# One transformer-like layer on one core: the Hyena filter's layers are placed ahead of the adaLN products in the first stage

## The chip, the cores and the metric

The kernel runs on one core of one Trainium2 chip. A core has five engines that run side by side, each with its own instruction queue, which it works off strictly in order: PE (TensorE, the matrix products), DVE (VectorE), ACT (ScalarE), POOL (GpSimd) and SP (SyncE, which here only issues transfers from memory to the core). The metric is the time of one execution on the device, in microseconds (us). Three executions of the kernel before took 1778.08, 1781.75 and 1783.15 us, so the median is 1781.75 us.

## The reference

The reference is one layer of a hybrid backbone over 512 latent tokens of width 1024, with 256 context tokens. Cut to what the change touches:

```python
mod = (silu(c) @ w_ada + b_ada).reshape(B, 1, 6, D)          # adaLN: shift, scale, gate, twice
xn = rmsnorm(x, norm_mix_g) * (1 + mod[:, :, 1]) + mod[:, :, 0]
cn = rmsnorm(ctx, norm_mix_g) * (1 + mod_c[:, :, 1]) + mod_c[:, :, 0]
p, pc = xn @ w_in, cn @ w_in                                  # one projection feeds three mixers
# the Hyena filter depends on weights alone, not on x
h = sin(freq[0] * (z @ f1_w + f1_b))                          # z: a table of positions, 512 x 33
h = sin(freq[1] * (h @ f2_w + f2_b))
h = (h @ f3_w).reshape(L, 2, 256) * decay[:, None, :]
K = rfft(concat(h[:, 0], 0, flip(h[1:, 1])))                  # used by the long convolution
# the RG-LRU's decay, from a parameter alone
log_a = -8 * r * softplus(-lam)
```

After this come neighbourhood attention, the Hyena convolution, the RG-LRU, a gated merge, an expert retrieval (PEER) over 16384 experts and a last RMSNorm.

## The kernel before, in words

The code is written once as a long program; a scheduler then sets, at build time, the order in which each engine gets its instructions (it moves an instruction ahead of others when it expects its inputs to be there), and the engines work off those fixed lists, waiting on semaphores. So the place of a piece of code moves work in the lists, but not one to one.

Activations lie transposed, as 8 blocks (index k, 0 to 7) of 128 features by 512 tokens. A product in full precision is made of three: each operand is split into a high part and a rest (`wh`, `wl` of a weight, `xh`, `xl` of the input), and `wh xh`, `wh xl`, `wl xh` are summed.

The first stage (before.py, lines 324 to 500) is one loop over k. Round k does the following.

- `mods(k)` (L422 to L439): two weight blocks `ada` of 512 KB each arrive (four buffers, so two rounds' worth), 8 products each of `silu(c)` with them go to the PSUM tile `hx`, ACT copies the result to `rows`, two small products with `pick` (L434) sum the partial rows, and DVE adds the bias (`mod`, L435) and makes the scale `gsx` (L437).
- In round 0 the input `xT` (four transfers of 512 KB) is squared on ACT (L298), summed on DVE (L300), summed over partitions by one product with `onesm` (L306), and turned into `rx`, one over the root mean square, by `rstd_of` (L231 to L237).
- In rounds 0 to 3 the weights of four of the input projection's column blocks arrive (`win`, 512 KB each) and are split by ACT and DVE.
- `norm_k` (L309 to L313): DVE scales `xT[k]` (L311), ACT adds the shift (`xh`, L312), DVE makes the rest (`xl`, L313).
- `part(k - 3)` (L443 to L447): the 12 products of input block k - 3 with those four weight blocks, 512 columns each. They accumulate over k in four PSUM tiles, so none is finished before `part(7)`.
- `filt()` (L371 to L411) is a generator that makes the Hyena filter in four pieces, one for each `next(fl)`: the first sine layer (L373, `sine` L335 to L349), the second (L377, and `softplus_rows`, a polynomial of some 25 tiny DVE operations for the RG-LRU), the third layer times the decay table (`hf`, `hp`, `hm`, L386 to L393), and the Fourier tables `Kf` (16 products of `dft` with the table `dftf`, L320, then L399 to L410). Before, the pieces run in rounds 1, 3 and 5 (`FS`) and after the loop. It uses `hx` tiles too, of which there are two.

After the loop, ACT copies the four finished tiles to `ha` (L271), ACT and DVE normalise the context, and the projections, the Hyena convolution and the RG-LRU begin. SP issues all transfers of the stage in one list; at most eight are under way, and a ninth waits for the landing of the first (the wait stands in SP's list).

Of the kernel before, what the change touches and what calls it, by code (L numbers as in the profile page):

```python
# [23 lines left out]
KD = 8  # L24
# [15 lines left out]
NFIRST = 4  # L40
SEQ1 = "hhhhrrhrrhhrhrhrhh"
SEQ2 = "vvvvrkrkrkrk"
FS = (1, 3, 5)
CS = 5
XK = 0
CL = 3
DL = 4
LAG = 3
NGR = 4
TWO_PI = 2.0 * math.pi  # L50
# [105 lines left out]
def emit(ctx, tc, A, out, dbg=None):  # L156
    nc = tc.nc
# [99 lines left out]
    dftf = hc.tile([128, 4, 2, 256], F32, name="dftf")  # L257
# [45 lines left out]
    def stats(npl, src, n):  # L303
        acc = ssq(npl, src, n)
        pss = hx.tile([128, 512], F32, name="hx")[:, :n]
        PE.matmul(pss, onesm, acc, start=True, stop=True)  # L306
        return rstd_of(npl, pss, n)
# [15 lines left out]
    with ExitStack() as st:  # L323
# [4 lines left out]
        zT = fp.tile([64, T], F32, name="zT")  # L328
        f1 = fp.tile([64, 64], F32, name="f1")
        f2 = fp.tile([64, 64], F32, name="f2")  # L330
# [20 lines left out]
        def softplus_rows():  # L351
            y = fp.tile([128, 4], F32, name="spy")
            z = fp.tile([128, 4], F32, name="spz")
            z2 = fp.tile([128, 4], F32, name="spz2")
            pl = fp.tile([128, 4], F32, name="spp")
            S.activation(y, vec("rlam"), AF.Abs)
            S.activation(y, y, AF.Exp, scale=-1.0)
            V.tensor_scalar(z, y, 2.0, None, ALU.add)
            V.reciprocal(z, z)
            V.tensor_mul(z, z, y)  # L360
            V.tensor_mul(z2, z, z)
            V.memset(pl, 1.0 / 19)
            for c in range(17, 0, -2):
                V.tensor_mul(pl, pl, z2)
                V.tensor_scalar(pl, pl, 1.0 / c, None, ALU.add)
            V.tensor_mul(pl, pl, z)
            V.tensor_scalar(y, vec("rlam"), -1.0, 0.0, ALU.mult, ALU.max)
            V.scalar_tensor_tensor(out=pl, in0=pl, scalar=2.0, in1=y, op0=ALU.mult, op1=ALU.add)
            V.tensor_scalar(nsp, pl, -8.0, None, ALU.mult)

        def filt():  # L371
            p = hx.tile([128, 512], F32, name="hx")
            PE.matmul(p[:64], f1, zT, start=True, stop=True)  # L373
            h1 = sine(p[:64], 0, vec("f1b")[:64])
            yield
            p = hx.tile([128, 512], F32, name="hx")
            PE.matmul(p[:64], f2, h1, start=True, stop=True)  # L377
            h2 = sine(p[:64], 1, vec("f2b")[:64])
            softplus_rows()
            yield  # L380
            hp = fp.tile([128, 4, 256], F32, name="hp")
            hm = fp.tile([128, 4, 256], F32, name="hm")
            for j in range(4):
                p = hx.tile([128, 512], F32, name="hx")
                o_ = j // 2 + 256 * (j % 2)
                PE.matmul(p, h2[:, o_:o_ + 255:2], f3, start=True, stop=True)  # L386
                hf = fp.tile([128, 2, 256], F32, name="hf", bufs=2)
                V.tensor_tensor(hf, p.rearrange("p (d c) -> p d c", d=2),
                                dec[:, j].unsqueeze(1).to_broadcast([128, 2, 256]), ALU.mult)
                if j == 0:  # L390
                    V.memset(hf[0:1, 1], 0.0)
                V.tensor_add(hp[:, j], hf[:, 0], hf[:, 1])
                V.tensor_sub(hm[:, j], hf[:, 1], hf[:, 0])  # L393
            yield
            for f in range(2):
                X, Y = hx.tile([128, 512], F32, name="hx"), at.tile([128, 512], F32, name="at")
                dft(X, Y, f, hp, hm)
                Ys = fp.tile([128, 512], F32, name="Ys", bufs=1)
                S.activation(Ys, Y, AF.Copy, scale=wf[:, f:f + 1])  # L399
                for i, op in enumerate((ALU.add, ALU.subtract)):  # L400
                    V.scalar_tensor_tensor(out=Kf[:, f, i, 0:512], in0=X, scalar=wf[:, f:f + 1], in1=Ys, op0=ALU.mult, op1=op)
                    if f == 0:
                        V.memset(Kf[0:1, 0, i, 256:512], 0.0)
                    S.copy(Kf[:, f, i, 512:768], Kf[:, f, i, 0:256])
                if f == 0:
                    V.tensor_scalar(Kq[:, 1], Ys[0:1, 256:512], 2.0, None, ALU.mult)
            p = hx.tile([128, 512], F32, name="hx")
            for k in range(2):
                PE.matmul(p[:32, :256], dftf[:, k, 1, 0:32], hp[:, k], start=k == 0, stop=k == 1)
            V.tensor_scalar(Kq[:, 0], p[0:1, :256], 2.0 / 1024, None, ALU.mult)  # L410
            yield  # L411

        fl = filt()
# [29 lines left out]
        def part(k):  # L443
            for i, (ps, wh, wl) in enumerate(first):
                PE.matmul(ps, wh[:, k], xh[:, k], start=k == 0, stop=False)
                PE.matmul(ps, wh[:, k], xl[:, k], start=False, stop=False)
                PE.matmul(ps, wl[:, k], xh[:, k], start=False, stop=k == KD - 1)  # L447

        for k in range(KD):
            lda = mods(k)  # L450
            if k == XK:
                for q in range(0, KD, 2):
                    nc.sync.dma_start(xT[:, q:q + 2], A["xT"][:, q:q + 2])
                rx = stats(npl, xT, T)
            if k == XK:
                for t_, n in ((zT, "zT"), (f1, "f1w"), (f2, "f2w"), (f3, "f3w")):
                    nc.sync.dma_start(t_, A[n])
            if k < NFIRST:
                src = A["win"][(14, 16, 15, 17)[k]]
                if k < 2:  # L460
                    w = load_raw(src)
                    wh, wl = (t[:, :, k * 128:k * 128 + 128] for t in (ch, cl))
                    S.copy(wh, w)
                    V.tensor_sub(wl, w, wh)
                else:
                    wh, wl = load_split(src)
                ps = (pj.tile([128, 512], F32, name="pj") if k < 2 else at.tile([128, 512], F32, name="at") if k == 2
                      else at.tile([128, 512], F32, name="po", bufs=1))
                first.append((ps, wh, wl))
            for q in (range(k + 1) if k == XK else [k] if k > XK else []):  # L470
                norm_k(xT, q, 0, gsx, rx, xh, xl)
            if k >= LAG:
                part(k - LAG)
            with tc.issue_after(lda.ins):
                if k == CL:
                    nc.sync.dma_start(cT, A["ctxT"])
                if k == DL:
                    nc.sync.dma_start(dec, A["dec"])
                if k == KD - 1:
                    for t_, n in ((wf, "wf"), (dftf, "dftf")):  # L480
                        nc.sync.dma_start(t_, A[n])
            if k in FS:
                next(fl)
            if k == CS:
                rc = stats(npl, cT, CT)
                V.tensor_tensor(cT, cT, rc.unsqueeze(1).to_broadcast([128, KD, CT]), ALU.mult)
# [830 lines left out]
```

## Time and profile before

| what | value |
|---|---|
| median of three runs | 1781.75 us (1778.08 to 1783.15) |
| the profiled execution's own time | 1777.03 us |
| its span, first to last instruction | 1774.9 us |
| what lies around the span | 2.1 us |
| PE busy | 1731.8 us (98%) |
| DVE, ACT, POOL busy | 1372.9, 788.6, 357.9 us |
| PE idle in all | 43.1 us |
| PE busy in the first 23 us | 9.35 us |
| mean granted TensorE clock | 0.995 |

The profiled execution is a run of its own, 4.7 us below the median and a little below the fastest of the three timed runs. The busy time of PE is modelled at the ends of products, so that a PE shown as full can still have small holes. The page names lines as they stand in before.py. In the changed file, lines from L44 on stand one to four lower or higher: the filter's L373 is L372 there, `mods` L429 is L427, `pick` L434 is L432, `part` L445 to L447 are L443 to L445.

### The profile page before, as it was taken

How to read it: one execution, taken by the hardware profiler on the slowest of the kernel's cores; microseconds unless marked ns; L12 is line 12 of the kernel's file. 1: busy time of each engine (PE TensorE's matmuls, PEld its weight loads, DVE VectorE, ACT ScalarE, POOL GpSimd, SP SyncE). 2: the span in 40 equal slices, each digit the busy share in tenths (PEclk: the TensorE clock that was granted, in tenths of full speed). 3: DMA queues.
4: the chain of work that ended last, by engine and by line, in shares of the span. 5: the costliest groups of instructions: out<-in, count | busy, mean ns of one | idle time of the engine just before them, and what ended most of it. 6: DMA issues, size and time to landing. Idle time of an engine off the chain costs nothing.

```text
span 1774.9 us, 25755 instructions
## 1 busy us (share of the span) xinstructions
PE 1731.8 (98%) x9601; PEld 1523.8 (86%) x9601; DVE 1372.9 (77%) x2555; ACT 788.6 (44%) x1140; POOL 357.9 (20%) x268
## 2 busy tenths in 40 slices
PE   6999999999999999999999999999999999999997
PEld 4778888888877889999999888888888888888885
DVE  7675666664448999999886787888888888788887
ACT  5545563343334235567766433333333333333334
POOL 0000000000000001100010233434434434444441
PEclk9999999999999999999999999999999999999999
DMA  9311155552343225767868999999999999999984
GB/s 343 105 60 60 48 167 172 186 172 87 119 163 119 84 86 189 257 223 287 290 253 323 376 353 344 338 330 341 337 353 341 348 343 349 332 345 339 321 287 150
DMA packets 157677, 431.33 MB, mean 243 GB/s; under 512 B 12784, under 2 KB 62192, under 8 KB 155504
## 3 DMA queue, kind: packets, MB, share of 16 engines
q1 hardware_dynamic: 116224, 257.44, 42.6%
q0 software_dynamic: 36864, 134.23, 20.9%
q10 hardware_dynamic: 4464, 38.01, 5.5%
q8 instruction: 75, 1.23, 0.3%
q14 instruction: 50, 0.41, 0.1%
HBM read 388.48 MB, written 41.16 MB: 242 GB/s over the span
## 4 chain that ended last, share of the span: by engine, by line
PE 85%; DVE 7%; DMA 4%; ACT 3%; issue 1%; SPq 0%; ACTq 0%; DVEq 0%
PE ac L1231 10%; PE ac L1232 10%; PE ac L1233 10%; PE pS L226 8%; PE pS L225 8%; PE pS L224 8%; PE pj L224 6%; PE pj L225 6%; PE pj L226 6%; DVE wl L218 2%; PE po L793 1%; PE pG L1104 1%; PE pG L1105 1%; PE hx L224 1%; PE hx L226 1%; PE hx L225 1%
## 5 line engine op out<-in xcount | busy, mean ns | idle before, releaser
L217 ACT CAST wh<-wraw 128x1024 fp32r<-128x1024 f32 x340 | 350.6, 1031 | 442.7 <-PE pS L225 227.2
L218 DVE TENSOR_TENSOR wl<-wraw,wh 128x1024 fp32r<-128x1024 f32 x340 | 406.7, 1197 | 140.3 <-ACT wh L217 138.8
L1132 POOL DMA_INDIRECT gr<-u_rows,idx x128 | 168.9, 1319 | 942.0 <-DVE db L1037 481.6
L226 PE MATMUL pS<-zh,wl 128*128 128x384 f32 x1024 | 345.6, 338 | 1.2 <-DVE wl L218 1.2
L224 PE MATMUL pS<-zh,wh 128*128 128x384 f32 x1024 | 344.7, 337 | 0.0
L225 PE MATMUL pS<-zl,wh 128*128 128x384 f32 x1024 | 344.6, 337 | 0.0
L1232 PE MATMUL ac<-wl,ah 128*128 128x512 f32 x768 | 299.0, 390 | 0.0
L1233 PE MATMUL ac<-wh,al 128*128 128x512 f32 x768 | 298.9, 389 | 0.0
L1231 PE MATMUL ac<-wh,ah 128*128 128x512 f32 x768 | 292.0, 389 | 0.0
L1142 POOL DMA_INDIRECT gr<-v_rows,idx x128 | 177.6, 1388 | 212.0 <-DVE yacc L1148 177.2
L224 PEld LDWEIGHTS pS<-zh,wh 128*128 128x128 f32 x1024 | 192.4, 188 | 3.0 <-ACT wh L217 0.5
L226 PEld LDWEIGHTS pS<-zh,wl 128*128 128x128 f32 x1024 | 192.3, 188 | 2.6 <-DVE wl L218 2.1
L225 PEld LDWEIGHTS pS<-zl,wh 128*128 128x128 f32 x1024 | 192.5, 188 | 2.3
L1233 PEld LDWEIGHTS ac<-wh,al 128*128 128x128 f32 x768 | 144.2, 188 | 30.0
L1231 PEld LDWEIGHTS ac<-wh,ah 128*128 128x128 f32 x768 | 144.2, 188 | 27.9
L1232 PEld LDWEIGHTS ac<-wl,ah 128*128 128x128 f32 x768 | 144.2, 188 | 27.8
L1148 DVE SCALAR_TENSOR_TENSOR yacc<-gr,cf,yacc 128x1024 f32<-128x1024 f32 x126 | 159.7, 1280 | 8.7 <-DMA gr<-v_rows,idx 8.6
L1134 DVE SCALAR_TENSOR_TENSOR gr<-gr,xtk 128x1024 f32<-128x1024 f32 x128 | 154.8, 1219 | 4.6 <-DMA gr<-u_rows,idx 4.6
L224 PE MATMUL pj<-xh,wh 128*128 128x512 f32 x336 | 134.8, 401 | 3.0 <-DVE ql L751 1.7
L226 PE MATMUL pj<-xh,wl 128*128 128x512 f32 x336 | 133.7, 398 | 1.0 <-DVE wl L218 1.0
L225 PE MATMUL pj<-xl,wh 128*128 128x512 f32 x336 | 133.8, 398 | 0.0
L1107 ACT COPY stg<-pG 128x512 f32<-128x512 f32 x96 | 99.4, 1164 | 23.9 <-PE pG L1105 23.7
(394 smaller groups left out, 2572.2 us busy)
## 6 DMA issues: line engine op xcount, KB each, us to landing
wraw<-u_cols SPq DMA_DIRECT2D x128, 512.0 KB, 6.3
wraw<-v_rows SPq DMA_DIRECT2D x128, 512.0 KB, 6.6
Gd<-stg ACTq DMA_DIRECT2D x12, 2048.0 KB, 8.9
gt<-Gd SPq DMA_DIRECT2D x32, 768.0 KB, 10.1
wraw<-wada SPq DMA_DIRECT2D x32, 512.0 KB, 4.4
wraw<-wgate SPq DMA_DIRECT2D x24, 512.0 KB, 3.5
Sd<-sg ACTq DMA_DIRECT2D x15, 768.0 KB, 4.9
sgl<-Sd SPq DMA_DIRECT2D x15, 768.0 KB, 7.9
```

The source lines that it names most:

```text
L217: S.copy(h[:, :k], r[:, :k])
L218: lsub[0] = V.tensor_sub(l[:, :k], r[:, :k], h[:, :k])
L224: PE.matmul(ps, wh[:, kw], xh[:, kx], start=start and j == 0, stop=False)
L225: PE.matmul(ps, wh[:, kw], xl[:, kx], start=False, stop=False)
L226: PE.matmul(ps, wl[:, kw], xh[:, kx], start=False, stop=stop and j == n - 1)
L1132: GP.indirect_dma_start(out=r, out_offset=None, in_=A["u_rows"], in_offset=bass.IndirectOffsetOnAxis(ap=idx3[:, j:j + 1], axis=0))
L1134: V.scalar_tensor_tensor(out=r, in0=r, scalar=1.0, in1=xtk, op0=ALU.mult, op1=ALU.mult, accum_out=sel3[:, j:j + 1])
L1142: GP.indirect_dma_start(out=r, out_offset=None, in_=A["v_rows"], in_offset=bass.IndirectOffsetOnAxis(ap=idx3[:, j:j + 1], axis=0))
L1148: V.scalar_tensor_tensor(out=a, in0=r, scalar=cf3[:, j:j + 1], in1=a, op0=ALU.mult, op1=ALU.add)
L1231: PE.matmul(ac[t][h], ah[:, ts], vhf[:, hs_], start=j == 0, stop=False)
L1232: PE.matmul(ac[t][h], ah[:, ts], vlf[:, hs_], start=False, stop=False)
L1233: PE.matmul(ac[t][h], al[:, ts], vhf[:, hs_], start=False, stop=j == NB - 1)
```

## The change

Four things change in the text of the first stage. The filter's small inputs (`zT`, `f1w`, `f2w`, `f3w`: 128, 16, 16 and 128 KB) are issued ahead of everything but `sv`. The decay table `dec` (512 KB), `wf` (1 KB) and the table `dftf` (1024 KB) are issued right behind `xT`, instead of behind the adaLN weights of rounds 4 and 7. The filter's four pieces run ahead of round 0, in round 0, and in rounds 1 and 3. `softplus_rows` leaves the second piece and is written in round 5.

```diff
-FS = (1, 3, 5)
+FS = (1, 3)
 CS = 5
 XK = 0
 CL = 3
-DL = 4
...
             h2 = sine(p[:64], 1, vec("f2b")[:64])
-            softplus_rows()
             yield
...
+        for t_, n in ((zT, "zT"), (f1, "f1w"), (f2, "f2w"), (f3, "f3w")):
+            nc.sync.dma_start(t_, A[n])
+        next(fl)
         for k in range(KD):
             lda = mods(k)
             if k == XK:
                 for q in range(0, KD, 2):
                     nc.sync.dma_start(xT[:, q:q + 2], A["xT"][:, q:q + 2])
+                next(fl)
                 rx = stats(npl, xT, T)
-            if k == XK:
-                for t_, n in ((zT, "zT"), (f1, "f1w"), (f2, "f2w"), (f3, "f3w")):
+                for t_, n in ((dec, "dec"), (wf, "wf"), (dftf, "dftf")):
                     nc.sync.dma_start(t_, A[n])
...
                 if k == CL:
                     nc.sync.dma_start(cT, A["ctxT"])
-                if k == DL:
-                    nc.sync.dma_start(dec, A["dec"])
-                if k == KD - 1:
-                    for t_, n in ((wf, "wf"), (dftf, "dftf")):
-                        nc.sync.dma_start(t_, A[n])
             if k in FS:
                 next(fl)
+            if k == CS:
+                softplus_rows()
```

What the scheduler made of it is seen in the engines' lists. From the end of the first context projection on, all lists are the same in both kernels, and no instruction is added; one table load of ACT is gone (the second L233). Three places matter.

SP's list from the start (`sv` is a table of small vectors, `wada` the adaLN weights, `win` the input projection's). Before:

```order
L176 DMA sv<-sv 128x156
L426 DMA ada<-wada 128x1024 x2
L453 DMA xT<-xT 128x1024 x4
L457 DMA zT<-zT 64x512
L457 DMA f_127<-f1w 64x64
L457 DMA f_128<-f2w 64x64
L457 DMA f_129<-f3w 64x512
L208 DMA wraw<-win 128x1024
L426 DMA ada<-wada 128x1024 x2
```

Changed:

```order
L175 DMA sv<-sv 128x156
L448 DMA zT<-zT 64x512
L448 DMA f_127<-f1w 64x64
L448 DMA f_128<-f2w 64x64
L448 DMA f_129<-f3w 64x512
L424 DMA ada<-wada 128x1024 x2
L454 DMA xT<-xT 128x1024 x4
L458 DMA dec<-dec 128x1024
L458 DMA wf<-wf 128x2
L458 DMA dftf<-dftf 128x2048
L207 DMA wraw<-win 128x1024
L424 DMA ada<-wada 128x1024 x2
```

Four small transfers now stand ahead of the first adaLN weights, and 1.5 MB of tables ahead of the first projection weights.

DVE's list while it sums the squares of `xT` (`sqa` the sum, `sk` and `sa` the sine's steps, `spp` and `nsp` the polynomial). Before:

```order
L435 TENSOR_TENSOR mod<-hx,sv 128x2x2
L300 TENSOR_TENSOR sqa<-sqa,sq 128x512
L368 SCALAR_TENSOR_TENSOR spp<-spp,spy 128x4
L437 SCALAR_TENSOR_TENSOR gsx<-mod,sv 128x1
L300 TENSOR_TENSOR sqa<-sqa,sq 128x512
L369 TENSOR_SCALAR nsp<-spp 128x4
L300 TENSOR_TENSOR sqa<-sqa,sq 128x512 x5
L464 TENSOR_TENSOR cl<-wraw,ch 128x8x128
```

Changed:

```order
L299 TENSOR_TENSOR sqa<-sqa,sq 128x512 x2
L433 TENSOR_TENSOR mod<-hx,sv 128x2x2
L340 TENSOR_SCALAR sk<-sa 64x512
L435 SCALAR_TENSOR_TENSOR gsx<-mod,sv 128x1
L341 TENSOR_SCALAR sk<-sk 64x512
L299 TENSOR_TENSOR sqa<-sqa,sq 128x512
L344 SCALAR_TENSOR_TENSOR sa<-sk,sa 64x512
L299 TENSOR_TENSOR sqa<-sqa,sq 128x512
L344 SCALAR_TENSOR_TENSOR sa<-sk,sa 64x512
L299 TENSOR_TENSOR sqa<-sqa,sq 128x512
L345 TENSOR_SCALAR sa<-sa 64x512
L299 TENSOR_TENSOR sqa<-sqa,sq 128x512 x2
```

The second sine layer's five steps now stand between the sums of the squares; the polynomial still stands ahead of both, as before, and the first sine layer's five steps now stand among its operations.

PE's list at the end of the stage (the last rows of `part(6)`, then `pick` of round 7, then the first rows of `part(7)`). Before:

```order
L446 MATMUL po<-xl,wh 128x512
L447 MATMUL po<-xh,wl 128x512
L320 MATMUL hx<-hp,dftf 128x256 x2
L320 MATMUL hx<-hm,dftf 128x256 x2
L320 MATMUL hx<-hp,dftf 128x256 x2
L320 MATMUL hx<-hm,dftf 128x256 x2
L445 MATMUL pj<-xh,ch 128x512 x2
```

Changed, first behind `part(3)` and then at the end:

```order
L444 MATMUL po<-xl,wh 128x512
L445 MATMUL po<-xh,wl 128x512
L427 MATMUL hx<-ada,ha_113 32x128 x32
L432 MATMUL hx<-pick,rows 128x2 x4
L305 MATMUL hx<-sqa,onesm 128x256
L427 MATMUL hx<-ada,ha_113 32x128 x16
L443 MATMUL pj<-xh,ch 128x512 x2
```

```order
L444 MATMUL po<-xl,wh 128x512
L445 MATMUL po<-xh,wl 128x512
L432 MATMUL hx<-pick,rows 128x2 x2
L443 MATMUL pj<-xh,ch 128x512 x2
```

Before, `pick` of round 7 stands inside `part(6)` and eight filter products lie between it and `part(7)`; now nothing lies between. And `mods` of rounds 4, 5 and 6 stand together ahead of `part(4)`.

## Rows read from the trace of the kernel before

**Rows 1.** Busy time by stretch: us, PE busy, PEld, DVE, ACT, POOL, clock, DMA share, GB/s.

```profile
23.00:72.00 49.00, 47.63 (x348) 33.26 (x344) 34.69 (x76) 20.96 (x37) 0.00 (x0) 0.97 0.53 198
101.00:1775.00 1674.00, 1650.12 (x9050) 1465.52 (x9048) 1302.11 (x2378) 735.76 (x1051) 357.17 (x262) 1.00 0.70 245
```

**Rows 2.** The chain that ended last, 0 to 120 us: start, us, what.

```profile
4.21 9.29 DMA xT<-xT
13.51 6.65 DMA wraw<-win
...
69.60 0.23 PE pj L447
```

**Rows 3.** DMA issues up to 60 us: times issued, KB, us from issue to landing.

```profile
dftf<-dftf SPq DMA_DIRECT2D x1, 1024.0 KB, 7.0
...
f<-f3w SPq DMA_DIRECT2D x1, 128.0 KB, 7.9
sv<-sv SPq DMA_DIRECT2D x1, 78.0 KB, 1.9
```

**Rows 4.** Timeline of SP's queue: start, us taken to issue, what.

```profile
4.82 0.56 SPq L457 DMA_DIRECT2D zT<-zT  x1
```

**Rows 5.** Timeline, start of the stage: start, us, instruction, [idle before <-what ended it].

```profile
8.83 0.63 ACT L298 ACTIVATE sqa<-xT 128x512 f32<-128x512 f32 x1
...
15.79 2.07 PE L306 MATMUL hx<-sqa,onesm 128*128 128x512 f32 x2 [5.79 <-DVE sqa L300]
...
23.17 1.22 PE L445 MATMUL pj<-xh,ch 128*128 128x512 f32 x2
```

**Rows 6.** DVE's groups up to 75 us: times run | busy us, mean ns | idle before.

```profile
L311 DVE SCALAR_TENSOR_TENSOR xT<-xT,gsx,rs_r 128x512 f32<-128x512 f32 x8 | 6.0, 748 | 0.2
L300 DVE TENSOR_TENSOR sqa<-sqa,sq 128x512 f32<-128x512 f32 x7 | 4.8, 691 | 0.5 <-ACT sq L298 0.2
L218 DVE TENSOR_TENSOR wl<-wraw,wh 128x1024 fp32r<-128x1024 f32 x3 | 3.6, 1215 | 0.7 <-ACT wh L217 0.7
L300 DVE TENSOR_TENSOR sqa<-sqa,sq 128x256 f32<-128x256 f32 x7 | 2.9, 415 | 0.3
L345 DVE SCALAR_TENSOR_TENSOR sa<-sk,sa 64x512 f32<-64x512 f32 x4 | 2.7, 677 | 0.0
L388 DVE TENSOR_TENSOR hf<-hx,dec 128x512 f32<-128x512 f32 x4 | 2.7, 687 | 3.6 <-PE hx L386 3.6
L392 DVE TENSOR_TENSOR hp<-hf 128x256 f32<-128x256 f32 x4 | 1.7, 421 | 0.0
L435 DVE TENSOR_TENSOR mod<-hx,sv 128x4 f32<-128x4 f32 x8 | 1.3, 158 | 3.1 <-PE hx L434 3.1
L341 DVE TENSOR_SCALAR sk<-sa 64x512 f32<-64x512 f32 x2 | 0.8, 414 | 0.4 <-ACT sa L340 0.4
```

**Rows 7.** Timeline, end of the stage (a product of 32-bit floats is listed as two).

```profile
60.00 1.08 PE L429 MATMUL hx<-ada,ha 128*32 128x128 f32 x32
...
62.55 0.50 PE L434 MATMUL hx<-pick,rows 128*128 128x2 f32 x4
...
64.71 0.71 ACT L312 ACTIVATE xh<-xT,mod 128x512 fp32r<-128x512 f32 x1
64.84 1.03 PE L320 MATMUL hx<-hp,dftf 128*128 128x256 f32 x4
...
68.11 0.81 PE L445 MATMUL pj<-xh,ch 128*128 128x512 f32 x2
```

**Rows 8.** Tile `ada`, its one transfer issued at 42.8 us into an idle queue.

```profile
DMA to landing us min/median/max: 3.7/3.7/3.7
```

**Rows 9.** Busy time by stretch, at the two falls of the clock (columns as Rows 1).

```profile
90.67:94.08 3.41, 0.89 (x8) 0.70 (x6) 3.41 (x7) 1.53 (x2) 0.00 (x0) 1.00 0.44 154
94.08:100.91 6.83, 6.41 (x17) 4.88 (x18) 5.10 (x13) 1.83 (x3) 0.00 (x0) 0.50 0.21 77
22.40:25.81 3.41, 3.41 (x35) 1.92 (x28) 3.41 (x9) 2.10 (x4) 0.00 (x0) 0.50 1.02 410
```

## Prediction

> **What bounds the kernel now.** I read first the busy time by stretch. Behind the first stage PE is busy 1650 of 1674 us [rows 1]: what follows runs PE's list, which the change leaves as it is, so a stage that ends later or earlier should move the end by as much. From 23 to 72 us PE is nearly full too, 47.6 of 49 us [rows 1]; the room lies ahead of 23 us. I then read the chain of waits: up to 20.2 us it is made of transfers, `xT` until 13.5 us and projection weights behind it [rows 2], then of PE with short pieces of DVE and ACT. Last I read the timeline at both ends of the stage. PE waits 5.8 us for the sum of the squares, which is there at 15.8 us, and `part(0)` begins at 23.2 us [rows 5]; `part(7)` begins at 68.1 us [rows 7]. So the question is what the change does to these two times.
>
> **Head of SP's queue.** Four small transfers move ahead of the adaLN weights. One took 0.56 us to issue [rows 4]; four make 2.2 us, so the first weights land some 2 us later. Their data are in time for PE's first filter product: `sv`, alone in the queue, took 1.9 us [rows 3]. The tables `dec` and `dftf` (1.5 MB) move ahead of the first projection weights; at the 410 GB/s of the full queue [rows 9] they take 3.8 us. Those weights thus land about 3 to 4 us later than before, near 20 us. That is not what decides, as the next part shows.
>
> **DVE sums the squares later.** This is the main cost. A sine layer is five DVE operations: two of 0.68 us and three of 0.41 [rows 6], together 2.6 us. Two of them now stand ahead of the end of the sum. The first runs among the polynomial's operations; ACT's sine stands in ACT's list ahead of the copy `rows` and the squares, so the first square, at 8.8 us before [rows 5], moves to about 12.2. From the first sum, at 13.5, DVE has seven sums of 0.69, the second layer's 2.6 us and two operations of 0.16: 7.7 us, so the sum is there at 21.4 us, not 15.8. From there to `part(0)` it took 7.4 us before [rows 5]. The table load and the weight split of ACT that lay in it are now partly done by then, so I take 6.5: `part(0)` begins at 27.9 us, 4.7 later. Bounds: 1.5 later, if ACT's sine is out early enough for the squares to keep up with `xT`, and 7 later, if the late weights hold ACT as well.
>
> **DVE's next stretch.** Between DVE's first scaling of `xT` (about 27.1 us) and round 2's `mod` now lie the filter's third layer and the context's squares: 4 `hf` of 0.69, 8 `hp` and `hm` of 0.42, three weight splits of 1.2, three operations of `norm_k` of 0.75, seven sums of 0.42 and six small ones of 0.16 [rows 6], in all 15.9 us: until 43.0. PE's own list to that point is shorter: 24 products of `part(0)` and `part(1)` at 0.23 us [rows 2], two rounds of `mods` of 1.1, eight Fourier products of 0.41 (eight took from 64.84 to 68.11 us) [rows 7] and three of the third layer, twice as wide, of 0.8: 13.4 us, until 41.3. So the other Fourier products, which need `hx` tiles that this `mod` frees, begin at about 43.2.
>
> **PE from there.** Eight Fourier products, 3.3; `part(2)` and `part(3)`, 5.5; two narrow products for `Kq`, 0.8; `mods` of rounds 4 and 5, 2.2; four rows of `pick` and the context's sum, 1.2: 56.2 us. Now round 6's `mods` come, and their weights can be issued only when round 4's have been read, from 53.3 us on. A transfer into an idle queue lands 3.7 us after its issue [rows 8], so they come at 57.0, the second half 1.3 us behind: PE waits 1.5 us in all and is through at 58.9. `part(4)` and `part(5)`, `pick`, round 7's `mods` and `part(6)` take 9.7: 68.6. Then `pick` of round 7, and `part(7)` must wait for DVE and ACT to make `xh` of it: 2.9 us from the start of `pick` (62.55) to the end of `xh` (65.42) before [rows 7]. Before, eight Fourier products covered this; they are gone from there, so it stands open: 71.5 us. By the same prices the old stretch from 23.2 to 68.1 comes to 40 us and took 44.9; the rest is a low clock and small holes. I have counted most waits by name, so I add 1.4, about a third of that rest, as an estimate. **`part(7)` begins at 72.9 instead of 68.1 us: 4.8 us later.** Bounds: 0 (no such rest, an early sum) and 9.
>
> **Behind it.** The last filter work (`Kf` on DVE, its copies on ACT, `Kq` on PE) is gone from behind `part(7)`. DVE and ACT were waiting for each other there, so I take no gain, and let a gain of 1 us widen the low side. The polynomial still heads DVE's list, the saved table load lay where ACT waited; both count nothing.
>
> The sum is +4.8 us on the profiled execution: 1777.0 to 1781.8. That execution lies 4.7 us under the median, so for the median I say 1781.75 + 4.8 = **1786.5 us**, 0.27% more. About 0.3% (5.3 us) is what a measurement of this kernel can tell from no change, so this is, narrowly, no change.
>
> **Rivals.**
> 1. *The clock falls at a new wait* (slower). Ahead of `part(7)` PE now waits 2.5 us. Before, PE had 0.89 us of work between 90.7 and 94.1 us, waiting for the rest, and the granted clock was 0.50 (1.2 GHz) for the next 6.8 us [rows 9]. The 12 products of `part(7)` would then take 0.43 us each instead of 0.23: 2.4 us more, +7.2 in all, 1789 us. It decides if the new wait is as bare as that one; the 1.5 us at `mods` are broken by eight products. At 22.4 us the clock was low as well [rows 9], and that stays. The Trainium skill (TensorE: Matmul & The Clock Gate, section HAM oscillation) says that waits of the products for data bring the clock down again; by that rule the trace agrees at 94 us, and this rival would hold.
> 2. *The early start comes true* (lower). If the sines fit into DVE's holes and ACT's squares follow `xT`, `part(0)` begins near 23.2 as before, with the second layer and one third-layer product (0.8 us each) already done, and `Kq` (0.8) no longer behind `part(7)`: about -2.5 us; with the low clock at 22.4 and the wait near 94 us also gone, up to -7, 1775 us. For it: PE is idle early. Against: DVE runs its list in order, and the sums stand behind the sines.
> 3. *Each small transfer pays its whole latency in turn.* `sv` alone took 1.9 us [rows 3]; four in a row would hold the first weights 7.6 us instead of 2.2, +10.2, 1792 us. Against it: before, the last of the four, issued behind the others, landed 7.9 us after its issue [rows 3], under 2 us behind the last `xT`; so they overlap. The Trainium skill (DMA: Bandwidth & Descriptors, section Anatomy of one DMA) states, for GpSimd's path, a fixed cost of about 2.0 us per transfer, which speaks against small ones in front. By it the four would cost 8 us if they did not overlap; the trace does not bear that out.
> 4. *Nothing moves.* The polynomial is not moved in DVE's list at all, and if transfers alone set the stage, the order of the rest is indifferent: 0, 1782 us.
>
> **Chances.** The forecast (+2 to +7, 1783.5 to 1789) 0.53, a third of it above 5.3 us; rival 1, 0.22; rival 2, 0.12, a third of it beyond -5.3; rival 3, 0.03; rival 4, 0.10. So slower by over 0.3%: 0.18 + 0.22 + 0.03 = 0.43. Faster: 0.04. Same: 0.53. The range from 1779 to 1791.5 us leaves out most of rival 2, rival 3 and the outer end of rival 1.
>
> **What would show it.** In the changed profile the sum's product (`onesm`) should start near 21, not 15.8 us, behind DVE; `part(0)` near 28; `mods` of round 6 should wait for a transfer, and the first product of `part(7)` for ACT's `xh`, about 2.5 us, starting near 73; the first stage's delay should be found again, unchanged, at 101 us and at the end. I am wrong if `part(0)` begins before 25 us, if `part(7)` begins before 69, or if the delay there is not that at the end. A clock of 0.50 between 70 and 80 us would be rival 1.

## The result and the profile after

The changed kernel takes 1791.3 us in the median of six runs (1787.5 to 1797.5), the kernel before, run beside it, 1781.0 us (1778.1 to 1783.2). The ratio is 1.0063, with a 95% interval of 1.0046 to 1.0080: 11 us slower, between 8 and 14. The prediction was 4.8 us, 1786.5. A second set of six runs gave 1793.4 us against 1780.1, ratio 1.0068 (1.0053 to 1.0083), 12 us.

The profiled execution took 1797.5 us, the slowest of its six; its span is 1795.4 us, PE was busy 1745.2 us. The profiled execution of the kernel before, 1777.0 us, lay a little below its timed runs, so the two are 20 us apart, twice what the medians are: the rows show where time goes, the medians how much it is. First the chain of waits up to `part(0)` (start, us, what), to be read against [rows 2]:

```profile
4.33 5.17 DMA ada<-wada
...
9.52 10.23 DMA wraw<-win
...
19.78 1.04 ACT ch L464
...
20.84 1.28 ACT L232
22.13 0.70 ACT rs_r L232
...
25.82 0.73 ACT xh L311
...
26.59 1.18 PE pj L443 x2
```

SP issues the first projection weights only when an adaLN block has landed (9.5 us), they land at 19.75 us (before, ACT's split of them began at 16.35), ACT splits them (`ch`), loads its table and only then makes `rs_r`. `part(0)` begins at 26.6 instead of 23.2 us [rows 5], and the 3.4 us are those of the landing (19.75 against 16.35). The sum of the squares, which the prediction had held responsible, is late as well, but not last. The timeline of PE (start, us, instruction, [idle before <-what ended it]):

```profile
19.70 2.07 PE L305 MATMUL hx<-sqa,onesm 128*128 128x512 f32 x2 [5.78 <-DVE sqa L299]
...
23.63 1.13 PE L384 MATMUL hx<-f,sh 64*128 64x512 f32 x2
...
26.59 1.18 PE L443 MATMUL pj<-xh,ch 128*128 128x512 f32 x2 [1.29 <-ACT xh L311]
27.70 2.07 PE L384 MATMUL hx<-f,sh 64*128 64x512 f32 x2
...
48.55 1.11 PE L319 MATMUL hx<-hp,dftf 128*128 128x256 f32 x4
...
63.72 0.66 PE L427 MATMUL hx<-ada,ha 128*32 128x128 f32 x16 [1.25 <-DVE xT L310]
64.87 1.08 PE L427 MATMUL hx<-ada,ha 128*32 128x128 f32 x16 [0.49 <-DMA ada<-wada]
...
81.24 1.21 PE L443 MATMUL pj<-xh,ch 128*128 128x512 f32 x2 [2.42 <-ACT xh L311]
...
104.91 0.64 PE L544 MATMUL hx<-ident,hu 128*128 128x128 f32 x4
```

The sum's product ends at 21.8 us; the two paths to `rs_r` end within 0.4 us of each other. The waits for round 6's weights (1.25 and 0.49 us; DVE, which the first row names, had long been done) and for `xh` ahead of `part(7)` (2.42 us) are there as predicted. But `part(7)` begins at 81.2 us, 13.1 later than before [rows 7], and the first transposes of the Hyena convolution (`ident,hu`) at 104.9 instead of 90.9 us. Two rows of the kernel before for this, from its timeline:

```profile
16.35 1.04 ACT L463 CAST ch<-wraw 128x1024 fp32r<-128x1024 f32 x1 [1.62 <-DMA wraw<-win]
...
90.92 0.64 PE L546 MATMUL hx<-ident,hu 128*128 128x128 f32 x4
```

The rest is in the clock. Busy time by stretch (us, PE, PEld, DVE, ACT, POOL busy, granted clock, DMA share, GB/s), cut where the clock changed; the stretches left out are at 1.00:

```profile
23.26:26.67 3.41, 2.12 (x23) 1.08 (x15) 3.31 (x5) 2.14 (x3) 0.00 (x0) 1.00 1.02 399
26.67:40.33 13.66, 13.66 (x22) 6.33 (x23) 11.23 (x24) 4.57 (x8) 0.00 (x0) 0.50 0.78 306
...
64.22:71.05 6.83, 6.34 (x35) 4.70 (x29) 0.87 (x2) 0.59 (x2) 0.00 (x0) 0.50 0.36 143
...
81.29:84.70 3.41, 3.41 (x8) 2.74 (x9) 3.38 (x4) 0.51 (x1) 0.00 (x0) 0.50 0.00 0
```

From 26.7 to 40.3 us PE is busy without a break and at half rate (1.2 GHz); before, the low stretch there was 3.4 us long [rows 9]. Among the products of this stretch stand three of the third layer's four, whose operands fill 64 of the 128 rows (`64x512`; each product is listed as two): 2.07 us, as at 27.70. The first of the four took 1.13 us (23.63), for the clock had been up from 23.3 us; it fell behind the wait of 1.29 us ahead of `part(0)`. Two further low stretches stand behind the two later waits. (Ahead of the first record of the clock, here up to 23.3 us, the column says 1.00 in every kernel; a pair of 512-column products that takes 2.07 us, as at 19.70, shows the lower level, since it takes 1.02 to 1.13 at 1.00.) A second profile of the same kernel has no record of the clock ahead of 42.8 us, with products at half rate up to there, and again a fall at each wait:

```profile
66.69:73.51 6.82, 6.20 (x31) 4.75 (x29) 0.75 (x1) 0.45 (x2) 0.00 (x0) 0.50 0.34 137
...
83.75:87.17 3.42, 3.42 (x8) 2.74 (x9) 3.39 (x4) 0.51 (x1) 0.00 (x0) 0.50 0.00 0
```

### The profile page after: what moved, and what is told of

Same layout as the page of the kernel before. It is cut to its first block, busy times and chain, and to the rows that moved or that the text cites. A ratio compares the mean times of both kernels' runs of the same rounds, so it can differ in the third digit from the quotient of the medians.

```text
span 1795.4 us, 25752 instructions
## 1 busy us (share of the span) xinstructions
PE 1745.2 (97%) x9601; PEld 1532.0 (85%) x9601; DVE 1373.1 (76%) x2555; ACT 787.6 (44%) x1139; POOL 353.6 (20%) x268
## 4 chain that ended last, share of the span: by engine, by line
PE 89%; DMA 5%; DVE 4%; ACT 2%; issue 1%; SPq 0%; DVEq 0%; ACTq 0%
PE ac L1229 9%; PE ac L1230 9%; PE ac L1231 9%; PE pS L225 9%; PE pS L223 9%; PE pS L224 9%; PE pj L223 6%; PE pj L225 6%; PE pj L224 6%; PE pG L1102 1%; PE po L791 1%; PE hx L223 1%; PE pG L1103 1%; PE hx L224 1%; PE hx L225 1%; DVE wl L217 1%
```

## The experiments

Each kernel was timed in 5 to 12 runs beside the kernel before, in four sets; "x us slower" is the ratio's value on 1780 us.

**The changed kernel again** (`after_again`), no edit.

> The changed kernel once more, for a second profile. Theory 'delay': the first stage is late by the order of the work alone (sines between the sums, wait before part(7)); a profile with no more low clock than the kernel before then has part(7) at 72 to 74 us and a time of 1785 to 1787 us, and the profile at hand (part(7) at 81.2) was one bad execution. Theory 'clock': TensorE, left with less to do early, stays at half rate to about 40 us in every execution; then the products of part(0) and of the third layer again take 0.43 us and 2.07 us for two, the granted clock is 0.50 for over 10 us ahead of 42 us, part(7) comes at 76 to 82 and the time is 1789 to 1793 us.

1793.4 us; the two rows above are its own, `part(7)` at 83.7 us. The early low clock stands in both profiles, and theory "delay" falls; `part(7)` and the time lie a little beyond what "clock" had said.

**Transfers alone** (`transfers_only`), against the kernel before:

```diff
+        for t_, n in ((zT, "zT"), (f1, "f1w"), (f2, "f2w"), (f3, "f3w")):
+            nc.sync.dma_start(t_, A[n])
         for k in range(KD):
...
                 rx = stats(npl, xT, T)
-            if k == XK:
-                for t_, n in ((zT, "zT"), (f1, "f1w"), (f2, "f2w"), (f3, "f3w")):
+                for t_, n in ((dec, "dec"), (wf, "wf"), (dftf, "dftf")):
                     nc.sync.dma_start(t_, A[n])
```

(and `dec`, `wf`, `dftf` no longer issued in rounds 4 and 7)

> Only the transfers of the change (four small ones ahead of the adaLN weights, the two tables ahead of the projection weights); the four pieces of the filter and the polynomial stay where they were. Theory 'delay' and theory 'clock' both say the transfers are not what costs: xT lands 1.2 us later than before, the sum's product starts near 17, part(0) at 24 to 25, part(7) near 69.5, time 1782 to 1784 us. Rival 'transfers': the later projection weights (19.8 instead of 16.3 us) set the stage; then part(0) is at 26 to 27 and the time 1786 to 1791 us.

1785.0 us, ratio 1.0028 (1.0015 to 1.0040), 5 us slower. The timeline of ACT and PE, then the stretch behind the clock's first recorded rise:

```profile
11.59 0.37 ACT L432 COPY rows<-hx 128x256 f32<-128x256 f32 x1 [7.00 <-PE hx L429]
...
18.73 2.08 PE L306 MATMUL hx<-sqa,onesm 128*128 128x512 f32 x2 [5.71 <-DVE sqa L300]
...
20.85 0.69 ACT L233 ACTIVATE rs_r<-hx,eps 128x512 f32<-128x512 f32 x1 [1.79 <-PE hx L306]
...
26.32 0.79 PE L445 MATMUL pj<-xh,ch 128*128 128x512 f32 x1 [0.28 <-ACT xh L312]
```

```profile
36.37:390.00 353.63, 345.33 (x1982) 289.66 (x1975) 228.33 (x367) 172.50 (x301) 3.61 (x2) 1.00 0.37 119
```

The transfers do cost, and `part(0)` is where the rival had it, at 26.3 us; the time lies between the two forecasts. The path is another one than in the changed kernel: the adaLN weights are late, ACT's squares stand in its list behind the copy `rows` that needs them, the sum comes 2.9 us later than before without any sine in front of it, and here `rs_r` waits for the sum, not for the projection weights. The clock is up from 36.4 us only. So 3 us of late start need no sine layer.

**Sine layers alone** (`sines_only`), against the kernel before:

```diff
-FS = (1, 3, 5)
+FS = (5,)
...
+        next(fl)
         for k in range(KD):
...
+                next(fl)
                 rx = stats(npl, xT, T)
```

(the four small transfers stand at the head here too)

> Only the two sine layers go early (with their four small transfers at the head); the tables, the third layer and the Fourier products stay in their old rounds, so eight Fourier products again stand between the last pick and part(7). Theory 'delay': the sum's product at 20 to 21 us, part(0) near 27, no wait before part(7), which starts at 71 to 72: 1784.5 to 1786 us. Theory 'clock': the same order, but the products of the rounds behind 27 us run at half rate to about 40 us as in the changed kernel: part(7) at 74 to 77, 1788 to 1791 us.

1782.9 us, ratio 1.0018 (1.0007 to 1.0029), 3 us slower. The sum's product starts at 21.2, `part(0)` at 28.8 us, later than in the changed kernel, and yet this one costs least, less than either theory had said. Its low stretch is short (busy time by stretch):

```profile
29.02:32.43 3.41, 3.41 (x22) 2.04 (x22) 3.27 (x9) 1.45 (x2) 0.00 (x0) 0.50 1.00 381
32.43:97.28 64.85, 60.01 (x402) 45.64 (x400) 40.11 (x84) 29.08 (x55) 0.00 (x0) 1.00 0.43 157
```

**Fourier tables back behind the loop** (`fourier_last`), against the changed kernel:

```diff
-FS = (1, 3)
+FS = (1,)
```

> The changed kernel with its last filter piece (Fourier tables) asked for behind the loop again, as before; the order on PE then has eight Fourier products in the middle of the stage and eight and the two narrow ones behind part(7). Theory 'delay': the same sum near 19.7 and part(0) near 26.6 as in the changed kernel; 4 us of work leave the place ahead of part(7) and come behind it; the wait of 2.4 us for xh stays: time within 2 us of the changed kernel's. Theory 'clock': the low stretches of the changed kernel's start (26.7 to 40.3) are there too, so no more than 2 us are won either. Rival 1 of the prediction (the wait before part(7) decides): if that wait is gone here, 2.5 to 5 us are won.

1784.8 us, ratio 1.0023 (1.0013 to 1.0032), 4 us slower than before and 8 faster than the changed kernel of the same set. The scheduler put eight Fourier products back ahead of `part(7)`, and the waits for the weights and for `xh` are gone (timeline of PE, then busy time by stretch):

```profile
66.55 1.08 PE L427 MATMUL hx<-ada,ha 128*32 128x128 f32 x32 [0.33 <-DVE mod L433]
...
74.88 0.82 PE L443 MATMUL pj<-xh,ch 128*128 128x512 f32 x2
```

```profile
41.77:103.20 61.43, 55.80 (x440) 44.95 (x440) 35.45 (x74) 29.23 (x53) 0.00 (x0) 1.00 0.36 129
```

The early half rate is there as before the edit (to 41.8 us); no fall follows until 103 us. Both theories had given 2 us at most: they had missed that the cover comes back. Rival 1 had 2.5 to 5 us for that case, and 8 is more than the two waits make (4.2 us). The two low stretches behind the waits are gone as well; they held 9.75 us of PE's work at half rate (6.34 and 3.41 in the first profile), so at 1.00 some 4.9 us less, by an estimate from these rows. That the remainder is this is not shown.

**Keeping PE busy early** (`warm_after`), against the changed kernel; nothing is left out, the added products go into a PSUM tile that is overwritten later (they are written out here; the kernel has them in a small helper function):

```diff
+        for _ in range(5):
+            PE.matmul(po0[:, :128], onesm, onesm, start=True, stop=True)
         next(fl)
+        PE.matmul(po0, f3[:, :128], zT, start=True, stop=True)
...
                 next(fl)
+                for q in (4, 5, 6, 7):
+                    PE.matmul(po0[:, :256], onesm, xT[:, q, :256], start=True, stop=True)
                 rx = stats(npl, xT, T)
```

> The changed kernel with products added whose result nobody reads, in TensorE's early waits (five while the first transfers come, one behind the first filter product, four on xT ahead of the sum); every engine's list is otherwise the same. Theory 'clock' (TensorE is at its lower level to about 42 us because it had too little to do before): the products of part(0) and part(1) take 0.23 instead of 0.43 us, the Fourier products behind them start at 43 to 46 instead of 48.6 and 51 us, and the kernel is 3 to 6 us faster than the changed one: 1787 to 1790 us. Theory 'delay' (DVE's list sets the pace there): at most 1 us is won, 1792 us or more.

1790.4 us, ratio 1.0054 (1.0038 to 1.0070): 1 to 3 us under the changed kernel, inside the uncertainty of both. The clock did rise, and fell again (busy time by stretch):

```profile
17.69:21.10 3.41, 1.12 (x2) 0.30 (x2) 1.78 (x4) 1.37 (x3) 0.00 (x0) 1.00 1.01 407
21.10:41.58 20.48, 19.04 (x60) 9.15 (x61) 16.23 (x29) 9.41 (x15) 0.00 (x0) 0.50 0.81 317
```

It was up at 17.7, with PE busy 1.1 of the next 3.4 us it went down, and it then stayed down for 20.5 us although PE was busy for 19.0 of them. So too little early work alone does not hold it down to 41 us; something in those 20 us does.

**Filling the wait ahead of `part(7)`** (`fill7`), and **both additions** (`warm_fill`: this edit and that of `warm_after`), against the changed kernel:

```diff
                                    op0=ALU.add, op1=ALU.mult)
+            if k == KD - 1:
+                for _ in range(3):
+                    PE.matmul(ps[:, 260:508], onesm, rows[:, :248], start=True, stop=True)
             return ld
```

> The changed kernel with three products of 248 columns added between the last pick and part(7), in the wait for xh, whose result nobody reads. They can't shorten the wait. Rival 1 of the prediction (the clock falls at this wait): the granted clock stays 1.00 behind it, the products of part(7) take 0.23 us instead of 0.43, 1.5 to 2.5 us are won, about 1791 us. If the wait alone costs: no difference to the changed kernel (1793 us), or 0.5 us more for what the added products hold up.

> Both additions at once. Theory 'clock': the gains add up, 5 to 8 us off the changed kernel, 1785 to 1788 us, which leaves the 3 to 5 us over the kernel before that the order alone costs. Theory 'delay': not under 1791 us.

`fill7`: 1792.1 us, ratio 1.0064 (1.0047 to 1.0081); `warm_fill`: 1792.5 us, ratio 1.0056 (1.0039 to 1.0074). Neither differs measurably from the changed kernel. In `fill7`'s profile the filling worked (timeline of PE, then busy time by stretch):

```profile
78.05 1.52 PE L439 MATMUL hx<-rows,onesm 128*128 128x248 f32 x6 [0.32 <-DVE mod L433]
80.15 0.73 PE L446 MATMUL pj<-xh,ch 128*128 128x512 f32 x2 [0.57 <-ACT xh L311]
```

```profile
67.80:105.35 37.55, 32.24 (x193) 26.30 (x191) 22.40 (x44) 20.03 (x34) 0.00 (x0) 1.00 0.25 85
```

The clock stayed at 1.00 behind the wait, and no gain is seen: the wait for `xh` itself remains. The fall behind it would cost 1.7 us (3.41 us of work at half rate, an estimate), and the interval of 3 us to either side can neither show nor exclude that. In `warm_fill`'s profile the early low stretch stood again, to 41.4 us.

**The kernel before, kept busy early** (`warm_before`) and **filled in its own wait near 92 us** (`before_fillhu`, two products of 512 columns between the two groups of `ident,hu`), each against the kernel before (the first again written out):

```diff
+        for _ in range(10):
+            PE.matmul(po0[:, :128], onesm, onesm, start=True, stop=True)
         for k in range(KD):
...
                     nc.sync.dma_start(xT[:, q:q + 2], A["xT"][:, q:q + 2])
+                for q in range(8):
+                    PE.matmul(po0[:, :256], onesm, xT[:, q, :256], start=True, stop=True)
```

```diff
         for c in range(2):
             p = hx.tile([128, 512], F32, name="hx")
+            for _ in range(2 * c):
+                PE.matmul(p, onesm, us[0], start=True, stop=True)
```

> The kernel before with such products in the same waits (ten while the first transfers come, eight on xT; the scheduler then also shifts a few products of the rounds 0 to 3). Theory 'clock': it too was held at half rate ahead of 26 us; the sum's product takes 1.1 instead of 2.1 us, the eight-product groups of mods 0.5 instead of 1.1, and 2 to 4 us are won: 1776 to 1778 us. Rival: transfers and DVE set the pace there, the PE work at half rate was hidden, 0 to 1 us.

> The kernel before with two added products (512 columns, result unread) in its own wait for hu at 91.6 to 94.2 us, behind which the granted clock was 0.50 for 6.8 us. Theory 'clock': the clock stays 1.00 there, the 17 products behind take 0.23 instead of 0.43 us, 2 to 3.4 us are won: 1777 to 1778.5 us. Rival: DVE, which is late there, sets the pace, and nothing is won: 1780 to 1781 us.

1779.9 us, ratio 1.0001 (0.9990 to 1.0013), and 1779.6 us, ratio 0.9997 (0.9985 to 1.0010): nothing won. In the first the clock was up from 6.7 us, but fell for 6.8 us at 20.4; in the second it stayed up behind that wait. A low stretch taken away is not time won in these two places.

**Third layer padded to 128 rows** (`pad128`), against the changed kernel; the added rows are zero:

```diff
-        f3 = fp.tile([64, 512], F32, name="f3")
+        f3 = fp.tile([128, 512], F32, name="f3")
+        V.memset(f3[64:], 0.0)
+        h2p = fp.tile([128, T], F32, name="h2p")
+        V.memset(h2p[64:], 0.0)
...
-            h2 = sine(p[:64], 1, vec("f2b")[:64])
+            sine(p[:64], 1, vec("f2b")[:64], h2p[:64])
+            h2 = h2p
...
```

> The changed kernel with the third layer's two operands padded with zeros from 64 to 128 rows; PE's list is the same. In the changed kernel these four products (2.07 us each at half rate) stand among the products of part(0) and part(1), and the clock is at its lower level to 40 to 43 us though TensorE is busy without a break from 27 us on, also where it had been kept busy before. Theory 'narrow products' (it is these products of 64 rows that keep the clock low): the granted clock is 1.00 by 31 to 35 us, the Fourier products behind start 3 to 5 us earlier, 1787 to 1790 us. Rival 'only time' (the rows don't matter): low to 40 us or more again, 1790 to 1794 us.

1785.5 us, ratio 1.0028 (1.0018 to 1.0039): 5 us slower than before instead of 12. This is the experiment that decides. The lists of PE, ACT and SP are, but for the padded operand's name, those of the changed kernel; DVE's has two memsets more and a few set-up operations of the first 5 us in another order. Busy time by stretch, then the timeline of PE:

```profile
23.13:98.22 75.09, 63.78 (x479) 49.55 (x479) 50.12 (x100) 35.51 (x64) 0.00 (x0) 1.00 0.48 174
```

```profile
24.29 1.13 PE L388 MATMUL hx<-f,h2p 128*128 128x512 f32 x2 [0.59 <-DVE rs_t L233]
...
31.48 1.02 PE L388 MATMUL hx<-f,h2p 128*128 128x512 f32 x2
...
42.53 1.11 PE L319 MATMUL hx<-hp,dftf 128*128 128x256 f32 x4
...
57.72 0.65 PE L431 MATMUL hx<-ada,ha 128*32 128x128 f32 x16 [1.26 <-DVE xT L310]
...
72.42 0.73 PE L447 MATMUL pj<-xh,ch 128*128 128x512 f32 x2 [2.42 <-ACT xh L311]
94.90 0.64 PE L548 MATMUL hx<-ident,hu 128*128 128x128 f32 x4
```

The clock is at 1.00 from 23.1 to 98.2 us, a pair of the padded products takes 1.02 us, the Fourier products on `hx` start at 42.5 instead of 48.6 us, the same two waits are there, and `part(7)` begins at 72.4 us. The rise at 23.1 us is not the padding's doing, since the first padded product starts at 24.3 us and the changed kernel's clock rose at 23.3 us too; what differs from there on is that the clock did not fall ahead of `part(0)`. How the padded products go when the clock is low among them is seen in two profiles further below.

**Second sine behind the sum** (`swap`), against the changed kernel:

```diff
-                next(fl)
                 rx = stats(npl, xT, T)
+                next(fl)
```

> The changed kernel with the second sine layer asked for behind the statistics instead of ahead of them. Theory of the prediction (the sines between the squares' sums delay part(0)): the sum's product at 16.5 to 18 instead of 19.7 to 20.9 us, part(0) at 24 to 25.5 instead of 26.6 to 27.7, 1 to 3 us won in the time: 1789 to 1792 us. Rival: part(0) waits for transfers and the later stretch decides, so nothing is won, 1791 to 1794 us; a gain over 4 us would mean that the waits at the later adaLN weights and ahead of part(7), or the low clock behind them, are gone too, since the order of the rounds 3 to 7 shifts as well.

1793.0 us, ratio 1.0072 (1.0056 to 1.0089): nothing won. The sum came 0.9 us earlier, `part(0)` did not (timeline of PE, then busy time by stretch):

```profile
18.80 2.08 PE L305 MATMUL hx<-sqa,onesm 128*128 128x512 f32 x2 [6.11 <-DVE sqa L299]
...
26.59 0.80 PE L443 MATMUL pj<-xh,ch 128*128 128x512 f32 x1 [1.96 <-ACT xh L311]
...
38.57 1.13 PE L384 MATMUL hx<-f,sh 64*128 64x512 f32 x2
```

```profile
36.42:63.73 27.31, 26.30 (x224) 19.15 (x222) 15.00 (x37) 8.53 (x18) 0.00 (x0) 1.00 0.36 127
```

With the sum earlier, DVE splits the late weights (`cl`) between the steps of `rstd_of`. The sum starts at 18.8 us here and at 18.7 in `transfers_only`, which has no sine ahead of it: of the 3.9 us by which it was late in the changed kernel, 2.9 come with the transfers and 0.9 with the second sine. The sines between the squares are not the cost that the prediction made of them. The rows show one thing more. Here two of the third layer's products stand together ahead of 34 us and two behind 38; the clock came up between them, at 36.4 us, and the later ones, with their 64 rows, did not bring it down. It fell at both later waits again, and the earlier rise shows as no gain in time (the order of the later rounds differs too).

**Third layer in round 3, Fourier tables in round 5** (`third_late`), against the changed kernel:

```diff
-FS = (1, 3)
+FS = (3, 5)
```

> The changed kernel with the third layer in round 3 and the Fourier products in round 5 (both sine layers and all tables early, as in the changed kernel). Theory 'narrow products': without the third layer among part(0) and part(1) the granted clock is 1.00 by 33 us, as it was where the third layer stayed late; 1783 to 1787 us. Rival 'only time': low to 40 us as in the changed kernel, and the time within 2 us of 1785, where the Fourier products alone had been put back.

1786.0 us, ratio 1.0029 (1.0020 to 1.0038). Without the third layer among `part(0)` and `part(1)` the clock came up at 33.1 us, as "narrow products" said (busy time by stretch), but it fell at 70.7 us for 6.8 us, behind three short waits of PE (0.49, 0.33 and 0.65 us):

```profile
33.14:70.69 37.55, 36.23 (x291) 26.19 (x289) 21.21 (x49) 10.78 (x24) 0.00 (x0) 1.00 0.41 154
```

Its time lies in both theories' ranges, so only the clock tells them apart.

**Both repairs** (`pad_fourier_last`), **the padding in the kernel before** (`pad_before`, the edit of `pad128` there), and **the padded kernel again** (`pad128_again`). The first, against `pad128`:

```diff
-FS = (1, 3)
+FS = (1,)
```

> Both repairs at once: the third layer's operands padded to 128 rows (clock), and the Fourier tables asked for behind the loop again (waits at the later adaLN weights and ahead of part(7)). Theory 'two causes' (half of the changed kernel's loss is the low clock up to 41 us, the rest the two waits of together some 4 us): the clock is 1.00 from 23 to 30 us on, neither wait is there, and the kernel ends within 2 us of the kernel before, 1778 to 1782 us. Rival 'one cause' (without the low clock the waits are covered by later slack, or without the waits the low clock costs nothing): no better than either repair alone, 1784 to 1787 us.

> The same padding in the kernel before, where the third layer stood at 47 to 51 us at full clock. A control: theory 'narrow products among the first products' says that padding wins nothing here, 1779 to 1781.5 us. If it wins 3 us or more here too, padding helps for another reason than the place that the change gave to these products.

> The padded changed kernel once more, for a second profile. If the clock behind the two waits (near 58 and 70 to 72 us) is a matter of the earlier low clock, it stays 1.00 there again; if it was chance, a stretch of 0.50 appears at one of them and part(7) ends 1.7 to 3.4 us later than in the first profile. The early part: 1.00 by 23 to 30 us, part(7) at 72 to 75 us; 1783 to 1787 us.

1779.7 us, ratio 1.0000 (0.9989 to 1.0011); 1779.6 us, ratio 0.9999 (0.9989 to 1.0010); 1785.3 us, ratio 1.0031 (1.0021 to 1.0041). Together the two repairs take away the whole loss, and the padding wins nothing where the third layer stands late. Alone they took 7 and 8 of the 12 us, so they overlap by some 3. `pad_fourier_last`, by stretch and on PE's timeline:

```profile
30.80:95.65 64.85, 59.89 (x455) 47.77 (x453) 43.03 (x89) 31.68 (x60) 0.00 (x0) 1.00 0.42 152
```

```profile
27.05 0.95 PE L447 MATMUL pj<-xh,ch 128*128 128x512 f32 x2 [1.52 <-ACT xh L311]
...
68.92 0.82 PE L447 MATMUL pj<-xh,ch 128*128 128x512 f32 x2
```

And `pad128_again`, likewise:

```profile
33.81:61.12 27.31, 25.93 (x243) 20.31 (x241) 16.87 (x39) 10.08 (x22) 0.00 (x0) 1.00 0.49 167
61.12:64.53 3.41, 2.95 (x21) 2.15 (x22) 0.72 (x1) 0.37 (x1) 0.00 (x0) 0.50 0.67 264
```

```profile
76.45 0.73 PE L447 MATMUL pj<-xh,ch 128*128 128x512 f32 x2 [2.42 <-ACT xh L311]
```

With both repairs `part(0)` still begins at 27.1 us, 3.9 later than before, but `part(7)` only 0.8 later: what was done early (the third layer) is gone from later, and pays the late start back. In this profile the clock fell at 27.4 us, behind the wait ahead of `part(0)`, and was up again at 30.8, with two of the padded products still to come (31.25 and 32.57). In the second profile of `pad128` the clock came up 11 us later than in the first, at 33.8 us, with the last of the padded products still to come (34.33), and fell at the first wait, yet not at the second. With 64 rows, in the six profiles with the changed kernel's order at this place, it came up only behind the last of these products (in the first profile that one ended at 36.9 us, and the clock rose at 40.3). So the falls behind the waits do not follow from the early low clock; whether one comes varies.

## Why the prediction was right and wrong

- **Head of SP's queue: mechanism right, weight wrong.** The late weights (19.75 us, predicted "near 20") were said to be "not what decides". The chain of the changed kernel shows that they do: `part(0)` is late by the 3.4 us of their landing. The bound "if the late weights hold ACT as well" was the case. And the late adaLN weights alone, through the squares, put `part(0)` at 26.3 us in `transfers_only`.
- **DVE sums the squares later: wrong as the main cost.** The sum did slip (19.7 us; predicted 21.4, though 13.5 + 7.7 makes 21.2), but it ends alongside the weights' path, 2.9 of its 3.9 us come from the transfers, and taking a sine out from between the sums won nothing (`swap`).
- **DVE's next stretch: right.** Predicted 43.2 us for the Fourier products on `hx`; in `pad128`, without the low clock, 42.5. PE had no wait just ahead of them there, so its own list was by then as long as DVE's.
- **The two waits: right in size.** Predicted 1.5 and 2.5 us, measured 1.74 and 2.42. Taking them out of the padded kernel, with the moved Fourier products, wins 5.6 us (1785.3 to 1779.7). The late start that the forecast put first is paid back by the end of the stage.
- **The sum without the long low stretch: right in size.** `part(7)` was predicted at 72.9 us; `pad128` has it at 72.4, and at 76.5 in the profile in which the clock rose later and fell once. In time it is 5.0 and 5.5 us slower than before where the forecast said 4.8.
- **Behind it: right.** In `pad128` `part(7)` is 4.3 us late and the transposes of `hu` are 4.0 late; nothing is given back there. The polynomial stayed where it was and showed up nowhere.
- **The clock: the step that failed.** The prediction let the low clock at 22.4 us "stay" as it was, 3.4 us long, and allowed 1.4 us for holes and low clock together. In fact the third layer's four products, moved among `part(0)` and `part(1)`, kept PE at half rate to 40 to 43 us. Padding them gives 7 us back (1.0068 against 1.0028 and 1.0031), which is about what the forecast lacks. In the profiles 6 us of it are there when the Fourier products on `hx` begin (48.6 against 42.5 us; in the second profiles 50.9 against 45.2); what the padding does to the later falls of the clock, which came in some profiles and not in others, is open.
- **Rival 1** (the clock falls ahead of `part(7)`) came true in both profiles of the changed kernel, and a fall at round 6's weights besides, which the prediction had ruled out because eight products break that wait. But with the same 2.42 us wait no fall came in either profile of `pad128`, and filling it won nothing measurable. At 1.7 us by estimate it is too small to carry the difference, and what both falls cost together was not measured by itself. The Trainium skill (TensorE: Matmul & The Clock Gate, section HAM oscillation) says that waits for data bring the clock down; at this wait the trace agrees in two of these four profiles.
- **Rival 3** (each small transfer pays its latency): refuted; each landed 2.0 to 2.6 us after its issue, side by side, where the last had taken 7.9 [rows 3]:

```profile
f<-f3w SPq DMA_DIRECT2D x1, 128.0 KB, 2.6
...
f<-f2w SPq DMA_DIRECT2D x1, 16.0 KB, 2.0
```

  (DMA issues of the changed kernel: KB, us from issue to landing.) **Rival 2** (early start): no sign of it. **Rival 4** (nothing moves): excluded by the interval.

## What to carry to other kernels

When products of few rows are moved among the first products of a kernel, read the granted clock where they go, and price them at both levels together with everything that stands between them: the same list cost 7 us more with 64 rows than with 128. Before moving work away from a chain, look whether it is the cover of a wait there; here eight Fourier products hid 2.4 us for `xh`. And where two late paths meet, ask the chain which one ends last before you call one the cost.

## What the runs showed of the hardware

- In the changed kernel PE was busy 13.66 of 13.66 us at a granted clock of 0.50 (1.2 GHz). The Trainium skill (TensorE: Matmul & The Clock Gate, section What's actually happening) says that activity releases the throttle and calls the busy state the fast one; by that the trace disagrees here. What differs is the rows of the third layer's products. With 64 rows the clock was down to 40.3 to 42.8 us in all six profiles with the changed kernel's order at this place, also where it had been up before (23.3 to 26.7 us in the first, 17.7 to 21.1 in `warm_after`). With 128 rows it stood at 1.00 from 23.1 us (a rise ahead of these products), 33.8 and 30.8 us. What the chip counts is not shown.
- Products of 64 rows did not bring down a clock that was up: in `swap` the last two of them took 1.13 us each at 1.00, and in the kernel before all four stand at 42.7 to 51.2 us, at 1.00.
- A low clock is not a loss in itself: the kernel before, with its early products or those behind its wait at 92 us kept at 1.00, won nothing (1.0001 and 0.9997; in the first another low stretch, of 6.8 us, came at 20.4 us).
- The moment at which the clock first rises varies between executions of the same program: 23.1 and 33.8 us for `pad128`, 23.3 and 42.8 us for the changed kernel.
